# A hybrid attention layer on one core: the second column tile's later weights in a tile of their own, the norm's transposes two blocks later, and the fourth to sixth tiles' stacks asked for later

## The chip, the core and the metric

The kernel runs on one core of one Trainium2 chip. The metric is the device time of one execution in microseconds (us). Engines are named as in the profile: PE is the tensor engine, DVE the vector engine, ACT the scalar engine, POOL is GpSimd, and SP is the engine whose queue issues most of the DMAs. A program that names its queue in this order runs it in this order: each engine works through its own row of instructions, and waits in place when the next one isn't ready.

## What is computed

One encoder layer over 1024 tokens of 1024 features. The part that matters here is its first half:

```
h      = rmsnorm(x) * norm_mix
z      = h @ w_in                     # 2304 columns: 18 tiles of 128
a      = window attention             # 8 heads of 64, 2 key/value groups, |i-j| <= 128, a sink logit per head,
                                      # rotary embedding on the first quarter of each head's features
b      = 2-D neighbourhood attention  # 8 heads of 64, learned bias
x      = x + concat(rmsnorm(a), rmsnorm(b)) @ w_out
x      = x + (silu(conv3(n @ w_gate)) * (n @ w_up)) @ w_down,   n = rmsnorm(x)
out    = rmsnorm(x)
```

## The kernel before, in words

The activations lie transposed, features on partitions. The projection goes by column tiles m = 0 to 17 (class Project): a tile is two halves of 512 tokens, and a half is eight blocks, one for each 128 rows of `w_in`. A block is three matmuls, L172 to L174, since each fp32 operand is split in a high and a low part (`xgh`, `xgl`, `whi`, `wlo`). Tiles 0 to 2 are window attention's first group (keys and values, then two tiles of queries), tiles 3 to 5 the second group in the same way, and 6 to 17 the neighbourhood attention.

**The start.** The first two tiles run together, block by block as x arrives (L739 to L744); the page calls their accumulators `pj` (tile 0) and `o` (tile 1). Weights come in two pieces of four blocks. Each piece is a `raw` tile, from which ACT makes `whi` (L156) and DVE `wlo` (L157); the pool has two buffers for `raw` and three for each of `whi` and `wlo`. `squares` (L211, L213) adds up x squared meanwhile, on ACT and DVE. The third tile follows (accumulator `s`), and between its blocks PE does the norm's sums: eight transposes of the squares after the first block (L781), eight more that spread the result (L263) after the sixth, from which ACT makes `rstd1` (L788).

**Attention units.** Window attention goes in 16 units of one block of 128 queries: units 0 to 7 are the first group, 8 to 15 the second. A unit has four heads, j = 0 to 3. Each has one pair of score matmuls (L436), a masked minimum on DVE (L466), the exponential on ACT (L470), and then brings the probabilities, split in two fp16 parts, across: head 0 by a high part on ACT and a low part on DVE (`stage` or `hl`, L487) and a transposing DMA that SP issues (L492); head 1 likewise with POOL's help; heads 2 and 3 by transposes on PE (L498) and copies on ACT and DVE (L502). The value matmuls (L525) follow, and a last add on DVE into `mixa` (L540) ends the unit. PE's order is written by hand: between the pieces of units stand blocks of the following projection tiles, from a generator (`rest`).

**What follows a tile.** When a tile's two halves have been copied out (L269), its `post` is to be run, which issues: for every tile of the first six the rotation, that is DMAs to and from a folded copy and adds and products on DVE (L285 to L291); for a tile of keys and values a scaling of the values (L358 to L376) and stacks of the keys (L340 to L343); for a tile of queries `split_pair`, a product on ACT (L298), one on DVE (L300), a copy of one half to the other (L301), and two more DMAs (L303). `split_pair` makes two tiles: heads 0 and 1 of a unit read those of the first query tile, heads 2 and 3 those of the second. Its first tile's second half is filled by the last DMA, which has to wait for L301's, since that one reads the place it writes.

**When post is asked for.** `settle` runs at each block of the filler and decides this. Before, tile 3 was asked for at block 13 of tile 4 and issued behind the first tiles' stacks; tile 4 at block 3 of tile 5, tile 5 at block 3 of tile 6. All engines but PE are ordered by a list scheduler over what has been asked for, with priorities; `behind(name)` puts an instruction behind a marked one on the same engine without a wait between engines.

Of the kernel before, what the change touches and what calls it, by code (L numbers as in the profile page):

```python
# [14 lines left out]
F32R = mybir.dt.float32r  # L15
# [3 lines left out]
ALU = mybir.AluOpType  # L19
# [11 lines left out]
MASKED = 1e30  # L31


LAG, LATE = 3, 13
FILL0, FILL1 = 22, 12
RATES = [45, 49, 22, 22, 22, 22, 20, 18, 16, 14]
AHEAD = 4
# [26 lines left out]
def hybrid_layer(tc, xT, w_in, w_out, w_gate, w_up, w_down, small, sink, rpb, consts, rope, out):  # L64
    nc = tc.nc
    with ExitStack() as ctx:
# [14 lines left out]
        def big(name, tag, dt=F32):  # L81
            return lpool.tile([128, S], dt, name=name, tag=tag, bufs=slots[tag])
# [55 lines left out]
        mark = {}  # L138

        def behind(*names):  # L140

            stack = ExitStack()
            for n in names:
                stack.enter_context(tc.issue_after(mark[n].ins))
            return stack
# [4 lines left out]
            nc.sync.dma_start(raw, src)  # L150
            return raw

        def halve_w(raw):

            hi, lo = (wpool.tile([128, 4, 128], F32R, name=n, tag=n) for n in ("whi", "wlo"))
            mark["weights"] = nc.scalar.activation(hi, raw, AF.Copy)  # L156
            mark["weights low"] = (nc.gpsimd if mark.get("attention") else nc.vector).tensor_tensor(lo, raw, f32(hi[:, :, :]), op=ALU.subtract)  # L157
            return [(hi[:, j, :], lo[:, j, :]) for j in range(4)]

        def load_w(src):  # L160
            return halve_w(fetch_w(src))
# [27 lines left out]
        def split_scaled(src, scale, name, tag):  # L189
            hi, lo = big(name + "h", tag, F32R), big(name + "l", tag, F32R)  # L190
            nc.scalar.activation(hi, src, AF.Copy, scale=scale)
            nc.vector.scalar_tensor_tensor(lo, src, scale, f32(hi[:, :]), op0=ALU.mult, op1=ALU.subtract)
            return hi, lo

        def split16(src, tag):
# [8 lines left out]
        def squares(tiles, halves=1, scales=None):  # L204
            acc = None
            n = S // halves
            for k, t in enumerate(tiles):
                s2 = tmp("sq")
                for i in range(halves):
                    cols = slice(i * n, (i + 1) * n)  # L210
                    nc.scalar.activation(s2[:, cols], t[:, cols], AF.Square, scale=scales[k] if scales else 1.0)  # L211
                    if acc is not None:
                        nc.vector.tensor_tensor(s2[:, cols], s2[:, cols], acc[:, cols], op=ALU.add)  # L213
                acc = s2
            return acc

# [287 lines left out]
        def unit_window(g, b):  # L504

            cs, n = near(b), 128 * len(near(b))
            mask = cst[:, K_MA:K_MA + 384].rearrange("p (c w) -> p c w", w=128)
            mask = mask[:, cs[0] - b + 1:cs[-1] - b + 2]
            st, turn = {}, {}

            def q_step(j):
                def go():
                    if j % 2 == 0:
                        turns_of["p"] += 1
                        st[j // 2] = Rows(turns_of["p"] % 6 in SPARE_A)
                    ps, _ = scores(qa[g, j // 2][j % 2], ka[g], b)
                    turn[j] = st[j // 2].softmax(PATH_A[j], j % 2, ps, n, mask, nsink[:, 4 * g + j:4 * g + j + 1], cs[0] - b + 1)
                return go

            def v_step(i, k):  # L520
                def go():
                    if i + k == 0:
                        st["o"] = bank("o", "o")
                    for s in range(2):
                        nc.tensor.matmul(st["o"][:, 256 * k:256 * k + 256], va[g][:, cs[i]], st[k].tile[:, :, cs[i] - b + 1, s], start=i + k + s == 0,  # L525
                                         stop=s == 1 and i == len(cs) - 1, skip_group_check=True)
                    if k == 1 and i == len(cs) - 1:
                        leave()
                return go

            def leave():
                ot = apool.tile([128, 2, 128], F32, name="ot", tag="ot", bufs=1, padded_shape=[128, 4, 128])
                o4 = st["o"][:, :].rearrange("p (j w) -> p j w", w=128)
                for e in range(2):
                    me, other = slice(64 * e, 64 * e + 64), slice(64 - 64 * e, 128 - 64 * e)
                    nc.scalar.activation(ot[me], o4[other, e::2, :], AF.Copy)
                    if (g, b // 4) not in mixa:
                        mixa[g, b // 4] = big("mixa", "mix")
                    dst = mixa[g, b // 4][:, :].rearrange("p (i w) -> p i w", i=2)[me, :, b % 4 * 128:(b % 4 + 1) * 128]
                    nc.vector.tensor_tensor(dst, o4[me, e::2, :], ot[me, 0:2], op=ALU.add)  # L540

            return [q_step(j) for j in range(4)], [v_step(i, k) for k in range(2) for i in range(len(cs))], [lambda j=j: turn[j]() for j in range(4) if PATH_A[j] == "T"]

# [175 lines left out]
            p.w = [(hi[:, j, :], lo[:, j, :]) for j in range(4)]  # L719
        for k in range(2, 4):  # L720
            xts.append(load_x(k))
        for p in first:
            p.w += load_w(w_in[p.m, :, 4:8, :])
        for k in range(4, KT):
            xts.append(load_x(k))
        nc.sync.dma_start(cst, consts)
# [12 lines left out]
        for k in range(KT):  # L739
            if k > 1:  # L740
                xg[k] = split_scaled(xts[k], col(C_NMIX + k), "xg", "xg")
            for h in range(2):
                for p, ps in zip(first, banks):
                    block(ps[h], p.w[k], xg[k], h, k == 0, k == KT - 1)  # L744
# [27 lines left out]

        rstd1 = big("rstd1", "rstd")
        rest3 = (step for h in range(2) for step in product(ps3[h], third.w, xg, h))
        next(rest3)
        v1 = gains
        with tc.high_priority(offset=300):
            for h in range(2):
# [36 lines left out]
                stacks(job.m, job.t)  # L815
            done.add(job.m)

        def settle(age):

            while waiting and (len(waiting) > 1 or age >= (LATE if waiting[0].m == 3 else LAG)):  # L820
                m = waiting[0].m
                if live["op"] + needs(m) > slots["op"]:
                    break
                live["op"] += needs(m)
                with behind(*["stack", "low"] * (m == 3)):
                    waiting.pop(0).post()

        aux = {}
# [1 line left out]
        def rest():  # L830
            for i, job in enumerate(jobs[1:]):
# [3 lines left out]
                for n, _ in enumerate(job.run()):  # L835
                    yield True
                    if i == 0:
                        if n == 8:
                            with behind("copied"):
                                for p in first:  # L840
                                    make_stacks(p)
                        continue
                    if n == REST and i + 2 < len(jobs):
                        jobs[i + 2].load_rest()
                    settle(n)
                    if (i, n) in aux:
                        aux[i, n]()
                if i == 0:
# [5 lines left out]
                if isinstance(job, Project):  # L854
                    waiting.append(job)
                while len(waiting) > 2:
                    settle(0)
                    if len(waiting) > 2:
                        yield False

# [1048 lines left out]
```

## Time and profile before

| | |
|---|---|
| Time, median of 3 runs | 1028.28 us (1027.95 to 1029.38) |
| The profiled execution's own time | 1028.71 us |
| Its span in the trace | 1026.6 us |
| PE busy | 1009.0 us (98%) |
| DVE, ACT, POOL busy | 875.2, 675.8, 214.6 us |
| Granted TensorE clock, mean | 0.997 |

Times in the trace are us from the start of the span. "Idle before <-releaser" at the end of a timeline row is the time for which the engine stood still ahead of it and what let it go on; a row with "x8" stands for eight like instructions. The 2.1 us between span and time lie outside the trace. Window attention's first units begin at 58 us, unit 8's scores at 118 us.

### The profile page before, as it was taken

How to read it: one execution, taken by the hardware profiler on the slowest of the kernel's cores; microseconds unless marked ns; L12 is line 12 of the kernel's file. 1: busy time of each engine (PE TensorE's matmuls, PEld its weight loads, DVE VectorE, ACT ScalarE, POOL GpSimd, SP SyncE). 2: the span in 40 equal slices, each digit the busy share in tenths (PEclk: the TensorE clock that was granted, in tenths of full speed). 3: DMA queues.
4: the chain of work that ended last, by engine and by line, in shares of the span. 5: the costliest groups of instructions: out<-in, count | busy, mean ns of one | idle time of the engine just before them, and what ended most of it. 6: DMA issues, size and time to landing. Idle time of an engine off the chain costs nothing.

```text
span 1026.6 us, 15663 instructions
## 1 busy us (share of the span) xinstructions
PE 1009.0 (98%) x5102; PEld 577.2 (56%) x5102; DVE 875.2 (85%) x1715; ACT 675.8 (66%) x1242; POOL 214.6 (21%) x339
## 2 busy tenths in 40 slices
PE   8999999999999999999999999999999999999996
PEld 6877777777775555544444444444444444444446
DVE  6799997767898799999897989888888879999865
ACT  7667787768687687645777777844544656655551
POOL 2225545777976210001000000000000000000002
PEclk9999999999999999999999999999999999999998
DMA  8566564786799874201787777723232778978734
GB/s 318 194 134 134 111 141 102 154 160 134 141 190 226 287 254 165 82 1 42 258 279 248 262 242 250 246 99 128 87 122 89 256 250 306 309 242 269 257 141 164
DMA packets 143938, 191.79 MB, mean 187 GB/s; under 512 B 77360, under 2 KB 88112, under 8 KB 143856
## 3 DMA queue, kind: packets, MB, share of 16 engines
q1 hardware_dynamic: 133264, 164.84, 56.2%
q10 hardware_dynamic: 10592, 25.95, 6.6%
q8 instruction: 40, 0.66, 0.3%
q14 instruction: 42, 0.34, 0.1%
HBM read 132.81 MB, written 28.57 MB: 157 GB/s over the span
## 4 chain that ended last, share of the span: by engine, by line
PE 75%; DVE 3%; DMA 2%; ACT 1%; issue 0%; POOL 0%; DVEq 0%; ACTq 0%; POOLq 0%
PE pj L180 7%; PE dn L1199 6%; PE dn L1198 6%; PE dn L1197 6%; PE z L1197 5%; PE z L1198 5%; PE z L1199 5%; PE x L1197 4%; PE y L1197 4%; PE x L1198 4%; PE y L1198 4%; PE y L1199 4%; PE x L1199 4%; PE pj L172 3%; PE pj L174 2%; PE pj L173 2%
## 5 line engine op out<-in xcount | busy, mean ns | idle before, releaser
L1199 PEld LDWEIGHTS <-wlo 128*128 128x128 f16 x898 | 87.9, 98 | 101.3
L1197 PEld LDWEIGHTS <-whi 128*128 128x128 f16 x898 | 88.1, 98 | 100.3
L1198 PEld LDWEIGHTS <-whi 128*128 128x128 f16 x898 | 87.9, 98 | 100.2
L1199 PE MATMUL dn<-xd,wlo 128*128 128x512 f16 (+1 forms) x330 | 120.4, 365 | 0.0
L1198 PE MATMUL dn<-xd,whi 128*128 128x512 f16 (+1 forms) x330 | 120.4, 365 | 0.0
L1197 PE MATMUL dn<-xd,whi 128*128 128x512 f16 (+1 forms) x330 | 120.4, 365 | 0.0
L172 PE MATMUL pj<-xgh,whi 128*128 128x512 f32 x248 | 106.8, 431 | 0.0
L1197 PE MATMUL z<-hg,whi 128*128 128x512 f16 x264 | 100.1, 379 | 0.0
L1198 PE MATMUL z<-hg,whi 128*128 128x512 f16 x264 | 100.1, 379 | 0.0
L1199 PE MATMUL z<-hg,wlo 128*128 128x512 f16 x264 | 100.1, 379 | 0.0
L470 ACT ACTIVATE p<-p,nm 128x385 f32<-128x385 f32 (+3 forms) x128 | 74.8, 584 | 35.7 <-DVE nm L466 27.1
L174 PE MATMUL pj<-xgh,wlo 128*128 128x512 f32 x248 | 97.7, 394 | 0.0
L173 PE MATMUL pj<-xgl,whi 128*128 128x512 f32 x248 | 97.4, 393 | 0.0
L1171 ACT ACTIVATE whi<-ws,m 128x512 f16<-128x512 f32 (+1 forms) x96 | 65.9, 708 | 35.6 <-DVE ws L1338 20.4
L1172 DVE SCALAR_TENSOR_TENSOR wlo<-ws,m,whi 128x512 f16<-128x512 f32 (+1 forms) x96 | 70.2, 741 | 17.9 <-ACT whi L1171 17.7
L1052 POOL TENSOR_TENSOR back<-back,cst 128x4 f32<-128x4 f32 (+1 forms) x7 | 2.8, 394 | 356.7 <-DVE back L1051 356.7
L1186 ACT ACTIVATE scan<-scan 128x1024 f32<-128x1024 f32 (+1 forms) x60 | 61.1, 1018 | 18.0 <-DMA scan<-in_w_down_dram 13.6
L1171 ACT ACTIVATE whi<-raw,m 128x512 f16<-128x512 f32 (+1 forms) x78 | 51.3, 699 | 17.7 <-DMA raw<-in_w_down_dram 9.6
L1172 DVE SCALAR_TENSOR_TENSOR wlo<-raw,m,whi 128x512 f16<-128x512 f32 (+1 forms) x78 | 55.4, 731 | 6.9 <-ACT whi L1171 6.9
L1197 PE MATMUL y<-hg,whi 128*128 128x512 f16 x160 | 60.6, 379 | 0.0
L1198 PE MATMUL y<-hg,whi 128*128 128x512 f16 x160 | 60.6, 379 | 0.0
L1199 PE MATMUL y<-hg,wlo 128*128 128x512 f16 x160 | 60.6, 379 | 0.0
(299 smaller groups left out, 2457.7 us busy)
## 6 DMA issues: line engine op xcount, KB each, us to landing
xd<-x SPq DMA_DIRECT2D x77, 256.0 KB, 5.5
raw<-in_w_down_dram SPq DMA_DIRECT2D x64, 256.0 KB, 3.6
x<-c ACTq DMA_DIRECT2D x22, 512.0 KB, 3.7
scan<-in_w_gate_dram SPq DMA_DIRECT2D x18, 512.0 KB, 4.5
scan<-in_w_up_dram SPq DMA_DIRECT2D x18, 512.0 KB, 6.1
raw<-in_w_gate_dram SPq DMA_DIRECT2D x18, 512.0 KB, 3.9
raw<-in_w_up_dram SPq DMA_DIRECT2D x18, 512.0 KB, 3.5
raw<-in_w_in_dram SPq DMA_DIRECT2D x32, 256.0 KB, 3.1
```

What stands on the lines that cost most here:

```text
L172: nc.tensor.matmul(ps, w[0], x[0][:, tsl(h)], start=first, stop=False)
L173: nc.tensor.matmul(ps, w[0], x[1][:, tsl(h)], start=False, stop=False)
L174: nc.tensor.matmul(ps, w[1], x[0][:, tsl(h)], start=False, stop=last)
L180: nc.tensor.matmul(ps, a, b, start=i == 0 and b is x[h][0] and a is w[0], stop=i == len(ws) - 1 and a is w[1])
L470: nc.scalar.activation(p[:, 0:e], p[:, 0:e], AF.Exp, bias=nm, scale=-1.0, accum_out=sm)
L1052: nc.gpsimd.tensor_tensor(back, back, unit_back.to_broadcast([128, n]), op=ALU.mult)
L1171: mark["whi"] = nc.scalar.activation(hi, src, AF.Copy, scale=by)
L1172: nc.vector.scalar_tensor_tensor(lo, src, by, hi, op0=ALU.mult, op1=ALU.subtract)
L1186: nc.scalar.activation(t, t, AF.Square, accum_out=dst)
L1197: nc.tensor.matmul(ps, w[0], x[0], start=first and i == 0, stop=False, skip_group_check=True)
L1198: nc.tensor.matmul(ps, w[0], x[1], start=False, stop=False, skip_group_check=True)
L1199: nc.tensor.matmul(ps, w[1], x[0], start=False, stop=last and i == len(ws) - 1, skip_group_check=True)
```

## The change

Three edits, and a fourth that goes with the first.

The later weights of tile 1 are no longer the fourth user of the three buffers of `whi` and `wlo`, but get a tile `wrest` in a slot of the pool of large tiles. On ACT its high part stands directly behind that of tile 0, five rows earlier than before; on DVE its low part stands directly behind that of tile 0, four rows earlier. The adds of `squares` are put behind the low part of the x tile two further on.

The norm's eight transposes come after the third block of the third tile and not after its first; so the eight that spread the result come two blocks later as well.

`settle` takes its moments from a table: tile 3 at block 10 of tile 5, tile 4 at block 1 of tile 6, tile 5 at block 7 of tile 6; and everything that these three issue goes behind the last L540 asked for by then.

```diff
-LAG, LATE = 3, 13
+LAG, DUE = 3, {3: (5, 10), 4: (6, 1), 5: (6, 7)}
...
-        def halve_w(raw):
+        def halve_w(raw, to=None):
-            hi, lo = (wpool.tile([128, 4, 128], F32R, name=n, tag=n) for n in ("whi", "wlo"))
+            hi, lo = to or (wpool.tile([128, 4, 128], F32R, name=n, tag=n) for n in ("whi", "wlo"))
...
-                        nc.vector.tensor_tensor(s2[:, cols], s2[:, cols], acc[:, cols], op=ALU.add)
+                        with behind(*[n for n in ("x low %d" % (k + 2),) if n in mark and k < 5]):
+                            nc.vector.tensor_tensor(s2[:, cols], s2[:, cols], acc[:, cols], op=ALU.add)
...
-                    nc.vector.tensor_tensor(dst, o4[me, e::2, :], ot[me, 0:2], op=ALU.add)
+                    mark["left"] = nc.vector.tensor_tensor(dst, o4[me, e::2, :], ot[me, 0:2], op=ALU.add)
...
-        for p in first:
-            p.w += load_w(w_in[p.m, :, 4:8, :])
+        first[0].w += load_w(w_in[first[0].m, :, 4:8, :])
+        rest = big("wrest", "mix", F32R)[:, :].rearrange("p (s k c) -> p s k c", s=2, c=128)
+        first[1].w += halve_w(fetch_w(w_in[first[1].m, :, 4:8, :]), (rest[:, 0], rest[:, 1]))
...
-        next(rest3)
+        for _ in range(3):
+            next(rest3)
...
-        def settle(age):
+        def settle(at, n):
-            while waiting and (len(waiting) > 1 or age >= (LATE if waiting[0].m == 3 else LAG)):
+            while waiting and (len(waiting) > 2 or (at, n) >= DUE.get(waiting[0].m, (at if len(waiting) > 1 else waiting[0].m + 1, 0 if len(waiting) > 1 else LAG))):
...
-                with behind(*["stack", "low"] * (m == 3)):
+                with behind(*["left"] * (m < 6)):
                     waiting.pop(0).post()
```

**First place, DVE at unit 0 and 1.** DVE's row before, from the first two minima of the first units. L287, L288 and L358 are tile 3's rotation and its values; L466 are minima of units 0 and 1, L269 a half of tile 4 copied out.

```order
L466 ISA nm 128x1
L287 TENSOR_TENSOR f<-f,turns 64x128 x2
L269 TENSOR_TENSOR t<-pj,rstd_370 128x512
L471 RECIPROCAL sm<-sm 128x1 x2
L466 ISA p,nm<-s,cst,nsink 128x384
L466 ISA nm 128x1
L484 TENSOR_SCALAR by<-sm 128x1
L288 TENSOR_TENSOR f<-f,turns 64x256
L358 TENSOR_REDUCE top<-t 64x1
L487 SCALAR_TENSOR_TENSOR hl<-p,by,hl 128x2x128
```

The same place now; line numbers are one higher from L213 on.

```order
L467 ISA nm 128x1
L472 RECIPROCAL sm<-sm 128x1
L270 TENSOR_TENSOR t<-pj,rstd_369 128x512
L485 TENSOR_SCALAR by<-sm 128x1
L472 RECIPROCAL sm<-sm 128x1
L467 ISA p,nm<-s,cst,nsink 128x384
L467 ISA nm 128x1
L488 SCALAR_TENSOR_TENSOR hl<-p,by,hl 128x2x128
```

Tile 3's rows are gone from here. They stand now, in the same order among themselves, from behind unit 0's last L540 on (unit 2's fourth minimum stands three rows ahead of that) to unit 4, and tile 4's rotation follows them where before it had stood among units 1 and 2.

**Second place, DVE at unit 7.** Before, between unit 7's third minimum and the part that it waits to bring across for its first head (L487 `stage`):

```order
L466 ISA p,nm<-s,cst,nsink 128x256
L466 ISA nm 128x1
L540 TENSOR_TENSOR mixa<-o,ot 64x2x128
L471 RECIPROCAL sm<-sm 128x1
L359 TENSOR_SCALAR top<-top 128x1
L487 SCALAR_TENSOR_TENSOR stage<-p,by,stage 128x2x128
L502 TENSOR_TENSOR turned<-pt,turned 128x3x128
```

Now, in the same place (L301 is tile 5's product, before at L300 and 32 rows ahead of this L487, in unit 6):

```order
L467 ISA p,nm<-s,cst,nsink 128x256
L467 ISA nm 128x1
L541 TENSOR_TENSOR mixa<-o,ot 64x2x128
L361 TENSOR_SCALAR top<-top 128x1
L362 RECIPROCAL down<-top 128x1
L301 SCALAR_TENSOR_TENSOR t<-t,q 128x1024
L488 SCALAR_TENSOR_TENSOR stage<-p,by,stage 128x2x128
L503 TENSOR_TENSOR turned<-pt,turned 128x3x128
```

Tile 5's product now comes after three of unit 7's four minima, directly ahead of the unit's `stage`. All DVE work of tiles 3 to 5 that stood ahead of this place before stands ahead of it now, but more of it stands behind unit 2's third minimum.

**Third place, SP's queue at units 6 to 8.** Before (names with numbers; q_1122 and q_1123 are tile 5's two stacks, `turned_1267` unit 6's first two heads, `turned_1384` unit 7's):

```order
L150 DMA raw_1357<-in_w_in_dram 128x512
L301 DMA q_1123<-q_1122 64x1024
L303 DMA q_1123<-t_779 64x1024
L303 DMA q_1122<-t_779 64x1024
L492 DMA_TRANSPOSE turned_1267<-hl_619 128x6x128
L492 DMA_TRANSPOSE turned_1267<-stage_618 128x6x128
L150 DMA raw_1648<-in_w_in_dram 128x512
L492 DMA_TRANSPOSE turned_1384<-stage_618 128x4x128
L492 DMA_TRANSPOSE turned_1384<-hl_619 128x4x128
```

Now (q_1200 and q_1201 are the two stacks, `turned_1266` unit 6's, `turned_1383` unit 7's):

```order
L493 DMA_TRANSPOSE turned_1266<-hl_618 128x6x128
L292 DMA t_748<-turns_169 16x8x128
L493 DMA_TRANSPOSE turned_1266<-stage_617 128x6x128
L150 DMA raw_1647<-in_w_in_dram 128x512
L302 DMA q_1201<-q_1200 64x1024
L304 DMA q_1201<-t_748 64x1024
L493 DMA_TRANSPOSE turned_1383<-stage_617 128x4x128
L304 DMA q_1200<-t_748 64x1024
L493 DMA_TRANSPOSE turned_1383<-hl_618 128x4x128
```

Tile 5's three DMAs moved behind unit 6's two transposes, and the last of them, which completes the stack that unit 8's third scores read, moved behind unit 7's first.

More of the change, by code (lines that the diff above doesn't have):

```diff
@@ L191, in split_scaled @@
             nc.scalar.activation(hi, src, AF.Copy, scale=scale)
-            nc.vector.scalar_tensor_tensor(lo, src, scale, f32(hi[:, :]), op0=ALU.mult, op1=ALU.subtract)
+            mark["split"] = nc.vector.scalar_tensor_tensor(lo, src, scale, f32(hi[:, :]), op0=ALU.mult, op1=ALU.subtract)
             return hi, lo
@@ L741, in hybrid_layer @@
                 xg[k] = split_scaled(xts[k], col(C_NMIX + k), "xg", "xg")
+                mark["x low %d" % k] = mark["split"]
             for h in range(2):
@@ L844, in rest @@
                         jobs[i + 2].load_rest()
-                    settle(n)
+                    settle(i + 3, n)
                     if (i, n) in aux:
@@ L856, in rest @@
                 while len(waiting) > 2:
-                    settle(0)
+                    settle(i + 3, 0)
                     if len(waiting) > 2:
```

## The prediction

> **What bounds the kernel now.** I read the page first, then PE's waits, then the timeline around each wait that the change touches. PE is busy 98% of the span, so a gain can only be a PE wait that goes.
>
> ```profile
> PE 1009.0 (98%) x5102; PEld 577.2 (56%) x5102; DVE 875.2 (85%) x1715; ACT 675.8 (66%) x1242; POOL 214.6 (21%) x339
> ```
>
> PE's waits by line and releaser (us in total, times, longest):
>
> ```profile
> PE o L525 <- DVE by L484: 1.4, 1, 1.4
> PE pt L498 <- POOL p L474: 1.4, 3, 0.7
> ```
>
> The first is a value matmul of window attention's first units; the second waits on the way from DVE over POOL. DVE is the engine to watch: from 80 to 117 us, where units 3 to 7 run, it has little room (columns: length, busy, instructions, clock, DMA share, GB/s).
>
> ```profile
> 80.00:117.00 37.00, 34.75 (x107) 1.00 0.66 136
> ```
>
> Idle there is 37.00 - 34.75 = 2.25 us.
>
> **First edit: tile 1's weights.** The timeline (start, duration, engine, line):
>
> ```profile
> 18.50 0.39 PE L173 MATMUL pj<-xgl,whi 128*128 128x512 f32 x1
> ...
> 18.73 0.39 PE L174 MATMUL pj<-xgh,wlo 128*128 128x512 f32 x1
> ...
> 19.19 0.61 ACT L156 ACTIVATE whi<-raw 128x512 fp32r<-128x512 f32 x1
> ...
> 19.86 0.50 PE L172 MATMUL o<-xgh,whi 128*128 128x512 f32 x1 [0.74 <-ACT whi L156]
> ...
> 20.04 0.69 DVE L157 TENSOR_TENSOR wlo<-raw,whi 128x512 fp32r<-128x512 f32 x1
> 20.20 0.40 PE L173 MATMUL o<-xgl,whi 128*128 128x512 f32 x1
> ...
> 20.79 0.50 PE L174 MATMUL o<-xgh,wlo 128*128 128x512 f32 x1 [0.20 <-DVE wlo L157]
> ...
> 21.12 0.40 PE L172 MATMUL pj<-xgh,whi 128*128 128x512 f32 x1
> ```
>
> Matmuls that don't wait start 0.23 apart (18.50, 18.73). From 18.73 to 21.12 are four such steps, 0.92 of 2.39: 1.47 us are lost. Now ACT makes the high part directly behind tile 0's and DVE follows: both are some 4 us early. Their 0.61 and 0.69 push x's next parts back by as much, ahead of the same amount taken out later; no `pj` or `o` matmul waits for those in this stretch, so I charge nothing, and 0.6 if one does. **-1.47** (-0.9 to -1.5).
>
> **Second edit: the transposes.** The last add of squares ends at 30.83, and the transposes follow at 31.37.
>
> ```profile
> 29.62 1.21 DVE L213 TENSOR_TENSOR sq<-sq 128x1024 f32<-128x1024 f32 x1
> ...
> 31.37 1.03 PE L781 MATMUL st<-cst,sq 128*128 128x128 f32 x8
> ```
>
> 0.54 us of slack is less than the 1.47 that PE gains, so unmoved they would wait 0.9; two blocks later (6 matmuls, 1.4 us) they reach 31.3 and don't. The same instructions, no time of their own: 0, and at most 0.5 if the add comes later too.
>
> **Third edit, what it frees: the first value matmuls.**
>
> ```profile
> 75.47 0.40 PE L174 MATMUL pj<-xgh,wlo 128*128 128x512 f32 x1
> 76.00 0.27 PE L525 MATMUL o<-turned,v 128*128 128x256 f16 x1
> 77.69 0.27 PE L525 MATMUL o<-turned,v 128*128 128x256 f16 x1 [1.42 <-DVE by L484]
> 77.80 0.51 PE L498 MATMUL pt<-cst,p 128*128 128x128 f32 x3
> ```
>
> 75.47 + 0.23 = 75.70, and the second L525 could follow the first by 0.11 (77.69 to 77.80): it starts at 77.69 instead of 75.81, 1.88 us late, behind this copy, which ends at 77.64:
>
> ```profile
> 77.25 0.39 DVE L502 TENSOR_TENSOR turned<-pt,turned 128x256 f16<-128x256 f32 x1
> ```
>
> DVE came to it so late because of these rows of tile 3:
>
> ```profile
> 59.59 0.48 DVE L287 TENSOR_TENSOR f<-f,turns 64x128 f32<-64x128 f32 x2
> ...
> 61.72 0.41 DVE L288 TENSOR_TENSOR f<-f,turns 64x256 f32<-64x256 f32 x1
> 62.15 1.22 DVE L358 TENSOR_REDUCE top<-t 64x1 f32<-64x1024 f32 x1
> ...
> 65.54 0.39 DVE L289 TENSOR_TENSOR f<-f 64x256 f32<-64x256 f32 x1
> ...
> 66.96 0.15 DVE L359 TENSOR_SCALAR top<-top 64x1 f32<-64x1 f32 x1
> ...
> 72.58 1.28 DVE L376 SCALAR_TENSOR_TENSOR vhl<-t,down,vhl 64x1024 f16<-64x1024 f32 x1 [1.01 <-ACT vhl L375]
> ...
> 74.98 1.21 DVE L342 TENSOR_TENSOR kb<-t,ka 64x1024 fp32r<-64x1024 f32 x1
> ```
>
> With five small rows such as L359's they are 5.7 us. Tile 4's two L287 and L288 move as well; like tile 3's (0.48 and 0.41) they are 0.9, a little more on twice the partitions: 6.7 together. They and the wait of 1.01 move behind unit 2, so the copy is no longer late: **-1.8** (-1.3 to -1.9). PE is then 1.47 + 1.8 = 3.25 us early at unit 2's third score.
>
> **Third edit, what it costs: tile 5's stack.** DVE's time is not saved but moved, behind the minimum that starts the first row here; the second row is unit 7's `stage`, which now has tile 5's product directly ahead.
>
> ```profile
> 79.59 0.62 DVE L466 CUSTOM_DVE_ANT_0 p<-s,cst,nsink 128x384 f32<-128x384 f32 x1
> ...
> 116.66 0.48 DVE L487 SCALAR_TENSOR_TENSOR stage<-p,by,stage 128x256 f16<-128x256 f32 x1
> ```
>
> Between them are 37.07 us, of which about 2.25 idle: 34.8 of work. With 6.7 more it is 41.5. The minimum follows its score, so it starts 3.25 early, at 76.3. So `stage` starts at 76.3 + 41.5 = 117.8 with no idle time at all, and at 120.1 with all of before's; I take 118.7, nearer the lower end, since added work fills idle time first, and 119.2 for its end. It can't use the time that it gains early (between 58 and 76 it now waits for PE), which is why a relief of 6.7 there brings PE 1.8 only.
>
> SP's queue, and the times from L303's issue to landing (shortest, median, longest):
>
> ```profile
> 105.96 0.49 SPq L301 DMA_DIRECT2D q<-q  x1
> 106.62 3.57 SPq L303 DMA_DIRECT2D q<-t  x2
> ...
> 117.21 1.19 SPq L492 DMA_TRANSPOSE turned<-stage  x1
> ```
>
> ```profile
> DMA to landing us min/median/max: 3.6/3.9/4.1
> ```
>
> Behind `stage` SP issues its transpose, 1.19, and only then the last DMA of tile 5's stack: 119.2 + 1.2 = 120.4, landing at 124.3 (by the ends above 123.1 to 125.9). The copy L301 ahead of it, which the last DMA also waits for, hangs on ACT's product, which stands behind the exponential of unit 7's first head: some 4 us ahead of `stage`, so that it lands no later than 120.4 (a like one took 3.75, from 105.96 to the second L303 at 106.62 + 3.57 - 0.48 = 109.71). The third score of unit 8 needs this stack. Before, PE came to it here, with the stack landed since 113.6 (109.71 and 3.9):
>
> ```profile
> 120.87 0.36 PE L436 MATMUL s<-ka,q 128*128 128x256 f32 x1
> ```
>
> So PE, which could be there at 117.6, goes on at 124.3: a wait of 6.7 in all, part of it already ahead at units 3 to 7, whose minima come late as well. At this point the kernel is 3.4 us later than before (2.2 to 5.0).
>
> The Trainium skill ("DMA: Bandwidth & Descriptors", Anatomy of one DMA — SWDGE (gpsimd) path) fits a DMA on GpSimd's path as about 2.0 us plus its bytes over 436 GB/s, for these 256 KB 2.6 us as an estimate; by it the delay would be 1.3 less. The trace has 3.6 to 4.1 for just this DMA on SP's queue, and that decides.
>
> **What is given back.** Later than before against DVE and POOL, PE finds ready what it waited for at 133 and 141 us (two of the three L498 waits):
>
> ```profile
> 133.31 0.55 PE L498 MATMUL pt<-cst,p 128*128 128x128 f32 x3 [0.26 <-POOL p L474]
> ...
> 141.40 0.55 PE L498 MATMUL pt<-cst,p 128*128 128x128 f32 x3 [0.70 <-POOL p L474]
> ```
>
> 0.26 + 0.70 = 0.96: **-0.9**. Behind that PE is the limit, and the shift stays to the end. Sum: 3.4 - 0.9 = +2.5 (1.3 to 4.1). The profiled execution took 1028.71, so 1031.2; it lies 0.43 above the median of 1028.28, against which I forecast **1030.8 us** (1029.6 to 1032.4).
>
> **The rivals.** *The gain stays.* If DVE's work in units 2 to 7 shrinks or its idle time takes the 6.7 up, tile 5's stack lands in time and 1.47 + 1.8 remain: 1025.0. Against it: 2.25 idle against 6.7. Half way, 4.4 of the 6.7 are taken up: the last DMA lands at 119.9, 2.3 late against 117.6, and 0.9 to 1.9 are left as gain (without and with what is given back): 1026.4 to 1027.4. I give 0.17 to gains over 0.2%, which is about what a measurement of this kernel can tell from no change (2.06 us).
>
> *About even.* DVE's jam is half of what I count, or the DMAs land at the short end: within 2 us of 1028.3. This holds the half-way case as well. 0.33.
>
> *The weights aren't early.* If PE waits at `o` for x's parts in place of weights (DVE has 0.69 more ahead of each), 0.6 of the 1.47 is lost; since unit 8 is set by DVE and SP, which start 0.6 later as well, 1031.4. Within the forecast's range.
>
> *Slower still, by the clock.* A PE that stands still for several us loses its clock. At the end of the span PE's last row is over at 1020.11; behind it the granted clock (the number behind PE's busy time and count) falls:
>
> ```profile
> 1019.49 0.62 PE L263 MATMUL sw<-cst,v 128*128 128x128 f32 x4 [0.64 <-DVE v L237]
> ```
>
> ```profile
> 1021.00:1022.00 1.00, 0.00 (x0) 0.64 0.39 131
> 1022.00:1023.00 1.00, 0.00 (x0) 0.50 0.82 267
> ```
>
> A stretch of 1 us with 0.64 is 0.72 of it at half speed: it halves some 1.2 us after the last matmul. No row shows how long it then stays low; if ten matmuls of 0.23 at unit 8 took twice as long, +2.3 would come on top of 2.5, 1033.1. It needs one wait of several us, while mine is spread over units 3 to 8. 0.10, in the slower share. The Trainium skill ("TensorE: Matmul & The Clock Gate", What's actually happening) has the clock drop after an idle window of about 3.4 us and come back after 3.4 us of work, which is 1.7 us lost as an estimate.
>
> **How the numbers follow.** Forecast with the clock's case 0.50 (0.40 and 0.10), about even 0.33, faster 0.17. The forecast's own ends, 1029.6 to 1032.4, hold some half of the chance; for eight in ten the range goes down through the even cases and the half-way gain to 1026.0 and up to the clock's 1033.1.
>
> **What would show it.** Right: no wait of PE at 19 to 21 us; the copy at 77 done before PE comes; DVE without gaps from 76 to 119; PE waiting at a score of unit 8 for the DMA `q<-t`, 3 us or more, or the same time in minima of units 3 to 8; the kernel behind before at 125 us and level from 150 on. Wrong: DVE gaps between 80 and 115, a stack that has landed by 118, or a shift that is still negative at 150 us.

## The result, and the profile after

The changed kernel takes 1035.36 us (median of 5 runs, 1035.10 to 1035.84), the kernel before 1028.34 in the runs beside it (1027.95 to 1029.38): a ratio of 1.0069 [1.0058, 1.0079]. It is slower, as forecast, but by 7.0 us instead of 2.5, outside the range. The profiled execution has a span of 1033.4 (before 1026.6) and a time of 1035.56. One of the six runs of e3 below took 1759.40 us at a mean granted clock of 0.556, the others 0.995 to 0.998; it is left out of e3's median and ratio.

How far TensorE is ahead (-) or behind (+) is read by laying the same score matmul of the two timelines side by side. The table gives, in us, its start minus that of the kernel before, for the kernels whose order tells something; records of kernels that are equal up to there differ by up to 0.7 in the first column, so differences along a row count.

| kernel | unit 0, first (before: 58.34) | unit 2, third (78.84) | unit 8, second (119.71) | unit 8, third (120.87) |
|---|---|---|---|---|
| prediction | -1.47 | -3.25 | not split | +3.4 |
| after | +0.22 | -1.19 | +3.95 | +6.69 |
| e1, first two edits | -0.23 | -0.22 | -0.22 | -0.22 |
| e2, third edit | -0.59 | -2.01 | +3.12 | +4.96 |
| e5, e1 and tile 4 early | -1.80 | -0.28 | -0.58 | -0.57 |
| e7, after and tile 4 early | -1.74 | -2.40 | +2.74 | +5.40 |
| e13, after, 1.9 us less DVE | -0.36 | -1.79 | +2.16 | +4.91 |
| e15, after, 3.7 us less DVE | -0.46 | -1.89 | +1.99 | +4.34 |
| e17, before, 2.7 us more DVE, spread | -0.31 | -0.30 | +1.10 | +1.10 |
| e18, before, 2.5 us more DVE, together | -0.38 | -0.35 | +1.34 | +1.33 |

PE's waits of after, by line and releaser (total, times, longest):

```profile
PE s L437 <- DMA q<-t: 2.5, 1, 2.5
PE o L526 <- DVE mixa L541: 1.9, 2, 1.5
PE pt L499 <- DVE turned L503: 1.5, 2, 1.1
PE pj L174 <- DVE wlo L157: 1.5, 1, 1.5
PE pt L499 <- POOL p L475: 1.4, 3, 0.7
...
PE s L437 <- DVE nm L467: 1.0, 1, 1.0
```

Five of the six are new, and four of these five have DVE as releaser. Five places tell what became of PE, in order of time.

*19 to 21 us.* The waits for the weights are gone, and matmuls follow each other by 0.23: from the first row here to the last are 0.91 us, and 2.39 before.

```profile
18.68 0.39 PE L174 MATMUL pj<-xgh,wlo 128*128 128x512 f32 x1
18.91 0.39 PE L172 MATMUL o<-xgh,wrest 128*128 128x512 f32 x1
...
19.59 0.39 PE L172 MATMUL pj<-xgh,whi 128*128 128x512 f32 x1
```

*57 us.* Here one wait takes all of that back: the matmul could have started at 55.64 + 0.23 = 55.87 and starts 1.65 later.

```profile
55.64 0.39 PE L173 MATMUL pj<-xgl,whi 128*128 128x512 f32 x1
...
56.78 0.68 DVE L157 TENSOR_TENSOR wlo<-raw,whi 128x512 fp32r<-128x512 f32 x1
...
57.52 0.50 PE L174 MATMUL pj<-xgh,wlo 128*128 128x512 f32 x1 [1.49 <-DVE wlo L157]
```

The same two rows in the kernel before:

```profile
56.21 0.68 DVE L157 TENSOR_TENSOR wlo<-raw,whi 128x512 fp32r<-128x512 f32 x1
...
57.43 0.39 PE L174 MATMUL pj<-xgh,wlo 128*128 128x512 f32 x1
```

DVE's row starts at 56.78 instead of 56.21: DVE was not early at all, and PE, which now was, met it.

*76 us.* The wait at the first value matmuls, 1.42 before, is 0.27:

```profile
75.96 0.27 PE L526 MATMUL o<-turned,v 128*128 128x256 f16 x1
76.50 0.27 PE L526 MATMUL o<-turned,v 128*128 128x256 f16 x1 [0.27 <-DVE turned L503]
```

*Units 3 to 7.* PE has room that it had not before, and DVE has almost none. The windows (length; busy time and number of PE, PEld, DVE, ACT, POOL; clock; DMA):

```profile
82.00:100.00 18.00, 15.08 (x85) 10.99 (x86) 17.55 (x52) 13.15 (x31) 9.83 (x20) 1.00 0.64 124
100.00:117.00 17.00, 15.55 (x92) 11.67 (x91) 16.47 (x51) 12.44 (x32) 8.59 (x18) 1.00 0.66 141
```

PE is idle for 2.92 and 1.45 us, DVE for 0.45 and 0.53. The waits of this stretch are 0.27, 0.49, 0.97, 1.46, 0.40 and 1.05. Two of the three longest (0.97 and 1.46) stand behind two rows of tile 3's that came here from 72 to 75 us, L377 and L343; the third (1.05, at 116.33) stands behind the maximum of tile 6, a row of 1.20 at 114.40:

```profile
92.16 1.28 DVE L377 SCALAR_TENSOR_TENSOR vhl<-t,down,vhl 64x1024 f16<-64x1024 f32 x1
...
93.47 0.56 DVE L503 TENSOR_TENSOR turned<-pt,turned 128x384 f16<-128x384 f32 x1
...
94.02 0.60 DVE L467 CUSTOM_DVE_ANT_0 p<-s,cst,nsink 128x384 f32<-128x384 f32 x1
...
94.54 1.21 DVE L343 TENSOR_TENSOR kb<-t,ka 64x1024 fp32r<-64x1024 f32 x1
94.68 0.44 PE L437 MATMUL s<-ka,q 128*128 128x384 f32 x1 [0.97 <-DVE nm L467]
...
97.44 0.43 DVE L541 TENSOR_TENSOR mixa<-o,ot 64x256 f32<-64x256 f32 x1
...
97.92 0.39 PE L526 MATMUL o<-turned,v 128*128 128x256 f16 x2 [1.46 <-DVE mixa L541]
```

The short rows that PE waits for (L503, L467, L541) queue behind each long one. From unit 2's third score to unit 8's second, PE falls back by 3.95 + 1.19 = 5.14.

*Unit 8's third score.* The chain that ends there:

```profile
118.30 1.06 ACT L299 ACTIVATE q<-t 128x1024 fp32r<-128x1024 f32 x1
...
119.38 0.47 SPq L302 DMA_DIRECT2D q<-q  x1
...
119.72 1.23 DVE L301 SCALAR_TENSOR_TENSOR t<-t,q 128x1024 fp32r<-128x1024 f32 x1
...
120.86 0.48 DVE L488 SCALAR_TENSOR_TENSOR stage<-p,by,stage 128x256 f16<-128x256 f32 x1
...
121.53 1.33 SPq L493 DMA_TRANSPOSE turned<-stage  x1
122.94 0.61 SPq L304 DMA_DIRECT2D q<-t  x1
...
127.57 0.36 PE L437 MATMUL s<-ka,q 128*128 128x256 f32 x1 [2.49 <-DMA q<-t]
```

ACT's half of the product, DVE's, the `stage` behind it, the transpose on SP, and only then the last DMA of tile 5's stack: 127.57 - 122.94 = 4.63 from its issue to the score. This is the mechanism that the prediction named, 3.3 us later than it said. The copy L302, which the last DMA must wait for too, was issued at 119.38 and had landed at 122.25 (the last mark of its semaphore in the trace). So it did not hold the last DMA; but without the transpose ahead of it that DMA could have gone only 0.7 earlier.

### The profile page after: what moved, and what is told of

Read it like the earlier page. It is cut to its first block, busy times and chain, and to the rows that moved or that the text cites. A ratio compares the mean times of both kernels' runs of the same rounds, so it can differ in the third digit from the quotient of the medians.

```text
span 1033.4 us, 15671 instructions
## 1 busy us (share of the span) xinstructions
PE 1010.6 (98%) x5102; PEld 578.1 (56%) x5102; DVE 876.6 (85%) x1715; ACT 676.8 (65%) x1242; POOL 213.0 (21%) x339
## 4 chain that ended last, share of the span: by engine, by line
PE 59%; DVE 5%; DMA 3%; ACT 1%; issue 1%; POOL 0%; SPq 0%; ACTq 0%; DVEq 0%; POOLq 0%
PE dn L1203 6%; PE dn L1201 6%; PE dn L1202 6%; PE pj L180 6%; PE z L1201 5%; PE z L1203 5%; PE z L1202 5%; PE y L1203 3%; PE x L1201 3%; PE y L1202 3%; PE x L1202 3%; PE x L1203 3%; PE y L1201 3%; DMA raw<-in_w_down_dram 1%; DVE wlo L1176 1%
## 5 line engine op out<-in xcount | busy, mean ns | idle before, releaser
L1203 PE MATMUL dn<-xd,wlo 128*128 128x512 f16 (+1 forms) x330 | 120.4, 365 | 0.0
L1202 PE MATMUL dn<-xd,whi 128*128 128x512 f16 (+1 forms) x330 | 120.4, 365 | 0.0
L1201 PE MATMUL dn<-xd,whi 128*128 128x512 f16 (+1 forms) x330 | 120.4, 365 | 0.0
```

The source lines that it names most:

```text
L1201: nc.tensor.matmul(ps, w[0], x[0], start=first and i == 0, stop=False, skip_group_check=True)
L1202: nc.tensor.matmul(ps, w[0], x[1], start=False, stop=False, skip_group_check=True)
L1203: nc.tensor.matmul(ps, w[1], x[0], start=False, stop=last and i == len(ws) - 1, skip_group_check=True)
```

## The experiments

**Which edit it is.** e1 holds the first two edits with the old moments, e2 the third edit alone.

```diff
 e2: -LAG, LATE = 3, 13
     +LAG, DUE = 3, {3: (5, 10), 4: (6, 1), 5: (6, 7)}
```

> The first two edits alone (the second tile's later weights, the squares' adds, the transposes two blocks later); the moments of tiles 3 to 5 as before. Theory A (the loss is tile 3's DVE work moved behind unit 2, and tile 5's last DMA): these edits cost nothing and bring nothing, because the 1.7 us that PE gains by 38 us are taken by one wait at 57 us for a low part of weights, which DVE makes after a row of rotations and stacks that starts no earlier than before: 1028.3 to 1028.7. Theory C (the weights edit itself loses, by the traffic and the wait at 57 us): 1029.5 or more. The prediction had 1026.8 for this part alone.

> The third edit alone (moments of tiles 3 to 5, all behind the last add of a unit); weights and transposes as before. Theory A: the whole loss, 1034.5 to 1035.5, with PE's waits in units 3 to 8 as in the changed kernel (about 8 us) and the wait at 77 us mostly gone. Theory C: clearly less than the changed kernel, 1034 or below.

e1 took 1028.39 us, ratio 1.0001 [0.9993, 1.0010]; e2 1034.41, 1.0065 [1.0053, 1.0077]. The whole loss is the third edit's, and the weights' gain reaches no unit: in e1, too, PE waits at 57.07 for the low part.

```profile
57.07 0.50 PE L174 MATMUL pj<-xgh,wlo 128*128 128x512 f32 x1 [1.34 <-DVE wlo L157]
77.47 0.27 PE L526 MATMUL o<-turned,v 128*128 128x256 f16 x1 [1.42 <-DVE by L485]
```

**Which tile's moment.** e3 puts tile 3 back to its old place and leaves tiles 4 and 5 late; e4 leaves tile 3 late and asks for tiles 4 and 5 earlier.

```diff
 e3: +LAG, DUE = 3, {3: (4, 13), 4: (6, 1), 5: (6, 7)}
     +with behind(*["stack", "low"] * (m == 3), *["left"] * (m in (4, 5))):
 e4: +LAG, DUE = 3, {3: (5, 10), 4: (5, 10), 5: (6, 3)}
     +with behind(*["left"] * (m == 3)):
```

> The changed kernel, but tile 3 asked for at block 13 of tile 4 and behind the first stacks, as before; tiles 4 and 5 late. Theory A: DVE has only tile 4's rotation (1.2 us) more behind unit 2, so the waits of units 3 to 7 nearly go, the wait at 77 us comes back by about 1, and unit 8's third score still waits 2 to 2.6 us for tile 5's last DMA: 1030 to 1031. Theory B (the late moments of tiles 4 and 5, on ACT's and SP's queues, make the loss, not DVE's load from tile 3): 1033 or more.

> The changed kernel, but tiles 4 and 5 asked for as soon as tile 3 has been, tile 5 at block 3 of tile 6 as before, and neither behind a unit's last add; tile 3 late. Theory A: DVE's jam in units 3 to 7 stays (about 5 us of PE waits) and the wait of unit 8 for the DMA goes: 1032 to 1033. Theory B: near the kernel before, 1028 to 1029.

e3: 1032.93, 1.0052 [1.0039, 1.0065]; e4: 1032.70, 1.0048 [1.0036, 1.0060]. The two losses, 1.0052 and 1.0048, add up to more than the whole: what the two groups of rows cost can't be added. In e3 the wait at 77 is back (1.23) and others stand at 113 (1.04) and 120 (1.90); in e4 the DMA's wait is gone, and PE waits three times from 91 to 108.

```profile
120.07 0.39 PE L526 MATMUL o<-turned,v 128*128 128x256 f16 x2 [1.90 <-DVE mixa L541]
```

```profile
91.59 0.55 PE L499 MATMUL pt<-cst,p 128*128 128x128 f32 x3 [2.23 <-POOL p L475]
97.20 0.44 PE L437 MATMUL s<-ka,q 128*128 128x384 f32 x1 [1.49 <-DVE nm L467]
107.87 0.38 PE L526 MATMUL o<-turned,v 128*128 128x256 f16 x2 [1.25 <-DVE mixa L541]
```

**The wait at 57 us.** e5 is e1, and e7 is after, each with tile 4's later weights taken out of their place behind the first stacks, so that the low part is made early.

```diff
-                    with behind("stack", "copied"):
+                    with behind():
```

> The first two edits alone, and tile 4's later weights no longer put behind the first stacks and copies, so that DVE makes their low part three long rows (4.9 us) earlier, ahead of the first keys' and queries' low parts. Theory A (the first edit's gain is real, and was taken by the wait for this one row at 57 us): that wait goes, the first scores come 0.6 to 1.4 us earlier than in the kernel before, and 0.5 to 1.4 us of it last: 1026.8 to 1027.7. Rival E (the first scores or the copy at 77 us are set by DVE's whole work, and the gain is only lost further on): 1028 to 1028.5.

> The changed kernel with tile 4's later weights early on DVE, as in the run of that edit alone. Theory A: the stretch from unit 2 to unit 8 is paced by DVE and takes as long as before, but begins 1 to 1.5 us earlier: 1033.8 to 1034.5. Rival E: as the changed kernel, 1035 to 1035.5.

e5: 1028.37, 1.0000 [0.9991, 1.0009]. PE comes to unit 0 1.80 us early, and of this 0.28 is left at unit 2's third score:

```profile
62.61 0.36 PE L437 MATMUL s<-ka,q 128*128 128x256 f32 x1 [0.30 <-ACT p L471]
74.29 0.44 PE L499 MATMUL pt<-cst,p 128*128 128x128 f32 x2 [0.67 <-DVE turned L503]
77.41 0.27 PE L526 MATMUL o<-turned,v 128*128 128x256 f16 x1 [1.22 <-DVE by L485]
```

e7: 1034.94 (1032.53 to 1035.32), 1.0058 [1.0045, 1.0072]. It comes to unit 2's third score 1.21 earlier than after and to unit 8's 1.29 earlier: a lead carries through units 3 to 8 one to one (2.74 + 2.40 = 5.14 lost up to unit 8's second score, as in after). Its median is hardly better for another reason, the clock, told at the end.

**Less DVE work.** e6 and e12 shorten the maxima in the sources of after and of before (1032.24, 1.0042 [1.0029, 1.0055]; 1030.35, 1.0021 [1.0012, 1.0030]). The program that orders the instructions then gave another order on every engine but PE, and before became slower with less work, so these two separate nothing. e13 to e16 therefore shorten rows in the finished program, with every engine's order as it was: two maxima in e13 (after) and e14 (before), from 1.2 to 0.3 each, these and the products of tiles 4 and 5, by 0.9 each, in e15 and e16. The maxima, and the low parts that the products make, then leave out all tokens but the first 128.

```diff
+    for b in nc.main_func.blocks:
+        b.instructions = [less(_dc, i) if i.name in LESS else i for i in b.instructions]
```

> The changed kernel, but with less work on DVE: the maxima of the values of tile 3 and later are taken over the first 128 of 1024 tokens (left out: the other tokens' maxima, so that the values are scaled by another power of two). Two of these reductions, of 1.2 us each, stand between unit 2's third minimum and unit 7's first part. Theory A (from there on DVE's work sets the time): each saves some 1.0, so that unit 7's part and tile 5's last DMA come 2 us earlier, and the time falls by 1.5 to 2: 1033.3 to 1034. Theory D (not DVE's work but the chain of handing over from ACT to SP, and the DMAs' own time, set unit 8): within 0.5 of the changed kernel, 1035.

> The kernel before with the short maxima (those of the values of tile 3 and later over the first 128 tokens only; left out: the other tokens). The same two rows of DVE are shortened by 1 us each as in the changed kernel, where this brought 3.1. Theory A: only tile 3's, at 62 us, stands ahead of a wait of PE (at 77 us), tile 6's at 113 us ahead of none: -0.8 to -1.1, 1027.2 to 1027.5. Theory G (the short maxima bring the same wherever they stand, so that what they brought in the changed kernel says nothing of the moved work): 1025 to 1026.

> The changed kernel with every engine's order as it is; in the finished program the maxima of tiles 3 and 6 run over the first 128 tokens only (left out: the other tokens), which takes two rows of DVE from 1.2 to some 0.2 us, both between unit 2's third minimum and unit 7's first part. Theory A (the amount of DVE work behind unit 2 sets the time): unit 7's part and tile 5's last DMA come 2 us earlier: 1033 to 1034. Theory D (the order, and what waits in it for other engines, sets it): 1034.6 to 1035.4.

> The kernel before with the same two rows shortened in the finished program, order as it is. Theory A: tile 3's row, at 62 us, stands ahead of the copy for which PE waits 1.9 at 77 us, so up to 1 comes off; tile 6's, at 113 us, stands ahead of no wait: 1027.3 to 1028. Theory D: no change, 1028.3. Were it slower, as with the short maxima that also changed the order (1030.4), less work itself would cost, which neither theory has.

> The changed kernel, order as it is, with four rows shortened: the two maxima, and tiles 4's and 5's products of 1.2 us, which run over the first 128 tokens (left out: the low parts of the other tokens' queries). 4 us less on DVE between unit 2's third minimum and unit 7's first part. Theory A: the stretch shrinks by 3 to 4, the waits of units 4 to 8 by as much: 1031 to 1032.5. Theory D: 1034 to 1035.4.

> The kernel before, order as it is, with the same four rows shortened. Theory A: in the kernel before the two products (at 85 and 105 us) stand ahead of no wait of PE longer than 0.5, so they bring 0 to 0.4 over the two maxima alone: 1027 to 1028.

e13: 1033.85 (1032.53 to 1035.68), 1.0059 [1.0046, 1.0072]; e14: 1028.06, 0.9999 [0.9990, 1.0008]; e15: 1032.76, 1.0050 [1.0038, 1.0063]; e16: 1028.28, 1.0000 [0.9992, 1.0009]. In before there is nothing to win. In after, units 3 to 8 lose 3.95 in e13 and 3.88 in e15 instead of 5.14, for 1.9 and 2.8 us less (the fourth row of e15, tile 5's product, stands behind the last of these waits): 0.6 and 0.45 of each us. Row by row it differs more. The maximum at 82 us takes away the wait of 0.49 at 89, that at 114 takes 0.71 off the wait of 1.05 at 116; tile 4's product at 108, shorter by 0.9 too, brings 0.07. The waits behind tile 3's two long rows are what they were (e13's line numbers are 14 higher):

```profile
93.61 0.45 PE L451 MATMUL s<-ka,q 128*128 128x384 f32 x1 [0.99 <-DVE nm L481]
96.85 0.39 PE L540 MATMUL o<-turned,v 128*128 128x256 f16 x2 [1.46 <-DVE mixa L555]
```

Those two rows themselves were not shortened: this would have left memory unwritten that is read later.

**More DVE work: amount or place.** e17 and e18 add four rows that nobody reads, 2.7 and 2.45 us in all, to the finished program of before: one ahead of each of four low parts, or all four ahead of one.

```diff
 e17: +LOW, AT = 180, {9: 1, 10: 1, 11: 1, 12: 1}
 e18: +LOW, AT = 180, {10: 4}
```

> The kernel before, whose finished program gets four extra VectorE rows of some 0.65 us (a maximum over 512 elements, read by nobody), 2.6 us in all: one ahead of each of the four weights' low parts at 82.6, 94.0, 103.7 and 110.8 us; the order of everything else is as before. Theory A (a row costs TensorE by how long it blocks the short rows behind it, so by its place and length): 0.65 at a time is mostly taken up, 1028.2 to 1029.2, with new TensorE waits under 0.6 each. Theory B (the prediction's: VectorE's total work in units 3 to 7 against its idle 2.25 there): 1028.3 to 1028.8, and the next run the same. Theory C (VectorE is full there, each us costs a us, wherever it is put): 1030.3 to 1031, and the next run the same.

> The kernel before with the same four extra VectorE rows of some 0.65 us, all four together ahead of the weights' low part at 94.0 us, in unit 5: a block of 2.6 us, as long as the two long rows of tile 3 that now stand at 92 to 96. Theory A: TensorE waits there for 1.0 to 2.5, and the run takes 1029.3 to 1030.8, at least 0.8 more than the one with the rows spread. Theory B: as the spread run, 1028.3 to 1028.8. Theory C: as the spread run, 1030.3 to 1031.

e17: 1029.44 (1028.93 to 1032.38), 1.0015 [1.0006, 1.0024]; e18: 1030.00, 1.0017 [1.0008, 1.0026]. By the table PE loses 1.40 spread and 1.69 together, 0.5 and 0.7 of each added us. So none of the three theories holds as written: place alone (A) wanted a gap of 0.8 between the two, the prediction's idle time (B) next to no loss, and a full DVE (C) all of 2.6. For these four rows the amount carries most of it and the place little (the single rows of e13 and e15 say otherwise); in e18 one block of 2.45 us ahead of many short rows becomes several small waits, none of them long. The longest:

```profile
112.30 0.39 PE L549 MATMUL o<-turned,v 128*128 128x256 f16 x2 [0.56 <-ACT turned L525]
```

**Ways to a faster kernel.** e8 is e5 with only tile 3's value halves and key stacks moved, behind the last copy of unit 1. e9 to e11 move low parts of the keys from DVE to POOL: tile 3's in before (e9), tile 3's and the first keys' in e5 (e10), the first keys' alone in e5 (e11).

```diff
 e8:  +LAG, LATE, LATER = 3, 13, (5, 8)
      +                    if (i + 3, n) == LATER:
      +                        with behind("crossed"):
      +                            while postponed:
      +                                postponed.pop()()
 e9:  -            nc.vector.tensor_tensor(b[e:e + 64], t[e:e + 64], f32(a[e:e + 64, :]), op=ALU.subtract)
      +            nc.gpsimd.tensor_tensor(b[e:e + 64], t[e:e + 64], f32(a[e:e + 64, :]), op=ALU.subtract)
 e11: +            nc.gpsimd.tensor_tensor(a[down], t[up], f32(a[up, :]), op=ALU.subtract)
```

> The kernel with the first two edits and tile 4's weights early, and of tile 3 only the last part late: the two halves of its values (DVE 1.28, behind a wait of 1.0) and the stacks of its keys (1.21) behind the last copy of unit 1's turned parts; its rotation and maxima as early as before, tiles 4 and 5 as before. Theory A: the wait at 77 us shrinks by about 1, and only 2.5 us are moved behind it, about what DVE has idle between 80 and 117 us (2.25), with some 7 us in hand for tile 5's stack: 1026 to 1027, 0.5 to 1 below the run without the split. Rival (DVE in units 3 to 7 can take nothing more): waits of 1 to 2.5 us in units 3 to 7, 1027.5 to 1029.

> The kernel before, with the low part of tile 3's keys (L342, 1.21 us on DVE, directly ahead of the copies that PE waits for at 77 us) computed on POOL, which is busy for 9 of the 23 us there; nothing is left out. Theory A (DVE paces this stretch, so work off it is time off): the copy comes 1 us earlier and the time falls by 0.7 to 1.1: 1027.2 to 1027.6. Rival F (POOL takes its place: its row of some 2.6 us stands ahead of the scaled probabilities that PE turns): 1028.3 to 1029.5.

> The first two edits and tile 4's weights early, with the low part of tile 3's keys and the second of the first keys' two low parts (L320, 1.22 us on DVE at 53 us) on POOL; nothing is left out. Theory A: the 1.8 us that are there at unit 0 and were lost at units 1 and 2 stay for the larger part, and the wait at 77 us shrinks: 1026 to 1027. Rival F: 1028.3 or more.

> As the run with both on POOL, but only the second of the first keys' low parts there; tile 3's on DVE as before. Theory A: the waits of 0.5 and 0.8 at units 1 and 2 shrink, the one at 77 us stays: 1027.2 to 1027.8. Rival F (the first scores wait for POOL's 2.6 us row instead): 1028 to 1029.

e8: 1032.10 (1030.15 to 1033.03), 1.0035 [1.0023, 1.0048]; e9: 1032.05, 1.0028 [1.0017, 1.0039]; e10: 1033.52, 1.0046 [1.0033, 1.0058]; e11: 1029.62, 1.0014 [1.0005, 1.0022]. None beats before. In e8 a PE wait of 3.02, up to 83.97, stands behind a POOL row of 1.57, the first of the two in the last line here; the second and the like one ahead of them took 0.58 and 0.59:

```profile
78.92 0.59 POOL L484 TENSOR_SCALAR p<-p,sm 128x384 f32<-128x384 f32 x1 [1.82 <-DVE sm L481]
...
82.34 2.13 POOL L484 TENSOR_SCALAR p<-p,sm 128x384 f32<-128x384 f32 x2
```

In e9 the key's low part takes 2.39 on POOL instead of 1.21 on DVE. DVE's row beside it, 0.29 in before, takes 1.89 and ends 0.16 behind POOL's, so DVE gained nothing; PE's wait at the value matmuls, 1.42 before, becomes 2.36.

```profile
73.72 2.39 POOL L342 TENSOR_TENSOR kb<-t,ka 64x1024 fp32r<-64x1024 f32 x1 [0.21 <-ACT ka L340]
...
74.38 1.89 DVE L287 TENSOR_TENSOR f<-f,turns 128x128 f32<-128x128 f32 x1
```

## Why the prediction was wrong

*The first edit, -1.47.* Right at its place: the waits at 19 to 21 are gone, 2.39 - 0.91 = 1.48. The second edit, 0: right, e1 shows nothing from it.

*What the third edit frees, -1.8.* Right in kind, -1.4 in size (0.22 to -1.19 in the table, with 0.27 of the wait left). Not all the rows named have a part in it: e14 shortens the maximum at 62 us by 0.9, and the wait at 77 stays 1.43.

*"PE is then 1.47 + 1.8 = 3.25 us early at unit 2's third score."* **This is the step that failed.** PE was 1.19 early (1.79 and 1.89 in e13 and e15, which are the same kernel up to there). The first term had been added as if nothing but the norm's transposes stood between 21 and 78 us; but at 57 us PE waits for DVE's low part of tile 4's weights, and DVE hadn't moved. The trace of before could have told: there that row ends only 0.54 us ahead of the matmul that reads it (56.21 + 0.68 = 56.89 against 57.43), so a lead of 1.47 does not fit past it. e5 and e7 show two things more. With this wait gone, a large part of the lead goes at the next waits of units 0 to 2: of 1.80 in e5 0.28 is left at unit 2's third score, of the 1.96 that e7 is ahead of after 1.21. And what is left there arrives at unit 8 one to one, as the prediction had it.

*The stretch from that minimum to unit 7's `stage`.* Predicted 118.7 - 76.3 = 42.4 us; measured 120.86 - 78.32 = 42.5:

```profile
78.32 0.62 DVE L467 CUSTOM_DVE_ANT_0 p<-s,cst,nsink 128x384 f32<-128x384 f32 x1
```

DVE's busy time in it (length; busy time and number; clock; DMA):

```profile
78.32:120.86 42.54, 40.74 (x123) 1.00 0.61 122
```

The size is right, but by two errors that cancel, so this was luck. DVE's work is 40.74, not 41.5: 5.9 more than the 34.8 before, not 6.7. Its idle time is 1.80, not 0.9: of 2.25 only 0.45 was filled, so here added work did not fill idle time first. That not each us counts alike is borne out: of 1.9 to 2.8 us taken out or put in, 0.45 to 0.7 come through (e13, e15, e17, e18), of the 6.7 moved 5.14, or 0.8. That these rows are long, and that two of them follow each other in one unit, may be the rest. e3 and e4, which don't add up, say that the order counts as well; how much of the 5.14 is amount and how much order is not settled.

*SP's queue and the landing.* The transposed part of the unit went as described, but the last DMA was issued 122.94 - 121.34 = 1.6 us behind `stage` instead of 1.2, and took 0.6 more to land than the 3.9 taken. The copy ahead of it landed at 122.25, not by 120.4: ACT's product ended only 1.5 ahead of `stage`, not some 4. That cost nothing here.

*What is given back, -0.9.* It was 0.4 (6.69 to 6.29 behind 134 us). The wait of 0.26 at 133 is gone, but that of 0.70 at 141 is as long as before, now at 147.68: what PE waits for there came late as well.

The sum: of 3.3 us that PE is later at unit 8's third score than predicted (6.69 against 3.4), 2.0 are the lead that was not there (78.32 against 76.3), 0.1 the stretch and the end of `stage`, 0.4 SP, and 0.7 the landing with the step from it to the score. With 0.5 that was not given back, 0.5 that came later still (span +6.8, behind 134 us +6.3) and 0.2 between profiled execution and median these are all but 0.1 of the difference of 4.6 in the forecast.

*The rivals.* "The gain stays" and "about even" needed DVE to take up all or half of the 6.7. Of the 6.7 moved 1.6 were taken up; in e17, of 2.7 added singly, half. "The weights aren't early" had the right suspicion at the wrong place. The clock's case did not occur in after (granted clock 1.00 through the wait of 2.49), but its price was seen in e7.

## What to carry to other kernels

A lead on one engine is worth nothing before it has been walked past every later row where that engine meets another one: list each meeting with its slack in the profile before, and stop the lead at the first whose slack is smaller. Work moved off a late engine into a stretch where this engine is 94% busy came back here at half to four fifths of its length taken together (single rows at 0.07 to 0.71 us for 0.9), whereas the place it left gives only what the other engine had waited there (1.4 of 6.7 here). And a DMA on whose landing a matmul depends should not be queued behind a transpose of the unit that runs at that time: here this cost up to 0.7 us.

## What was not expected of the hardware

*The clock after a wait of 2.4 us.* In e7 (and in e13) the granted clock, the number behind the fifth engine, fell to half behind the wait at unit 8, in e7 within 0.2 us of its end, in e13 1.2 us behind it. The windows of e7:

```profile
126.00:127.00 1.00, 0.72 (x3) 0.75 (x4) 1.00 (x2) 0.26 (x1) 0.66 (x1) 0.73 0.00 0
127.00:128.00 1.00, 1.00 (x4) 0.38 (x4) 0.97 (x2) 0.00 (x0) 0.85 (x3) 0.50 0.00 0
128.00:129.00 1.00, 1.00 (x6) 0.94 (x6) 0.21 (x2) 0.00 (x0) 0.00 (x0) 0.50 0.43 88
129.00:130.00 1.00, 1.00 (x5) 0.88 (x4) 0.48 (x3) 0.87 (x3) 0.18 (x1) 0.57 1.00 58
```

Ahead of it:

```profile
126.28 0.40 PE L437 MATMUL s<-ka,q 128*128 128x256 f32 x1 [2.41 <-DMA q<-t]
```

By these windows the clock is low for 3.4 us, and PE falls back from +5.40 at unit 8's third score to +6.98 at unit 9: 1.6 us. The one run of e7 at 1032.53 has a mean clock of 0.998, the other four, 2.2 to 2.8 us longer, 0.995 to 0.996. But a wait alone does not decide it: waits of 2.41 (e7) and 2.50 (e13) were followed by the low clock, while after with 2.49 and e8 with 3.02 keep 1.00 in their profiles. The Trainium skill ("TensorE: Matmul & The Clock Gate", What's actually happening) has the clock drop after an idle window of about 3.4 us that runs freely, and come back after as much work; it calls the transition run-variable. The 3.4 us until it came back agree, and so does the difference between runs; a wait of 2.4 us is shorter than the page's window.

*POOL beside DVE.* POOL's row of 128x384 takes 0.58 or 0.59 in most places, in e8 1.57 beside DVE's L343 (82.24 to 83.46), and in before 1.63 beside tile 5's product. Two runs tell whether that is the cause: e14 and e16 have the same order as before, and e16 shortens this product. The rows of e14, then of e16:

```profile
105.19 1.65 POOL L488 TENSOR_SCALAR p<-p,sm 128x384 f32<-128x384 f32 x1 [0.67 <-DVE sm L485]
...
105.25 1.23 DVE L312 SCALAR_TENSOR_TENSOR t<-t,q 128x1024 fp32r<-128x1024 f32 x1 [0.16 <-ACT q L310]
...
105.11 0.69 POOL L490 TENSOR_SCALAR p<-p,sm 128x384 f32<-128x384 f32 x1 [0.67 <-DVE sm L487]
...
105.13 0.30 DVE L312 SCALAR_TENSOR_TENSOR t<-t,q 128x128 fp32r<-128x128 f32 x1
```

With 0.93 less on DVE, POOL's row is shorter by 0.96: DVE's row is the cause of the longer time here. In e9 it is the other way round, where DVE's row takes 1.89 beside POOL's. The Trainium skill ("SBUF — State Buffer", Who interferes with whom) says that DVE and POOL share a pair of ports, and that an instruction holds it to its end; both cases agree with it. That the ports are what holds the row is not shown by a run.
